# A two-layer attention encoder step on one core: full-width low weights for the sample, scans at another pace and place, and a scale chain in pieces

## The chip, the cores and the metric

The kernel runs on one core of a Trainium2 chip. The metric is device time in microseconds (us) of one execution. A core has five engines that run side by side, each in its own order: TensorE (PE, matmuls; its weight loads are listed as PEld), VectorE (DVE), ScalarE (ACT), GpSimd (POOL) and SyncE (SP), on whose queue this kernel starts all of its DMA transfers. SBUF is the on-chip memory of 128 partitions; PSUM takes what PE makes.

## The reference

Two layers, each `x + W_out(attention(RMSNorm(x)) * silu(gate))`, over a prompt of 2048 frames and a sample of 64 frames that comes with cached keys and values.

```python
def project(x, norm_g, w_in, q_g, k_g, n_heads, n_kv):
    h = rms_norm(x, norm_g)
    p = h @ w_in
    ...
    q, k, v, gate = jnp.split(p, [wq, wq + wkv, wq + 2 * wkv], axis=-1)
    ...
def gated_attention_layer(x_p, x_s, ck, cv, norm_g, w_in, q_g, k_g, w_out, ...):
    qp, kp, vp, gp = project(x_p, norm_g, w_in, q_g, k_g, n_heads, n_kv)
    op = prompt_band_attention(qp, kp, vp, past_chunks, bias_fn, sinks)
    y_p = x_p + (op * jax.nn.silu(gp)) @ w_out
    qs, ks, vs, gs = project(x_s, norm_g, w_in, q_g, k_g, n_heads, n_kv)
    os_, nk, nv = sample_band_attention(qs, ks, vs, ck, cv, bias_fn, sinks)
    y_s = x_s + (os_ * jax.nn.silu(gs)) @ w_out
```

D_MODEL is 1024; layer A has 16 heads over 2 key/value heads and a band of 2 past chunks of 64 frames, layer B 16 heads and 8 past chunks. The outputs must be near fp32 accuracy.

## The kernel before

**Precision by parts.** Each operand is split into a high and a low part, and a product is made of high x high, high x low and low x high. Layer A uses fp32r parts. Layer B and the second output projection use f16 parts, which need scales (powers of two) that keep weights, activations and outputs within f16. These scales are made from the largest absolute values of `w_in_b` (64 pieces), `w_o_b` (16) and `cv_b` (4).

**Scans.** The 84 pieces, 128 x 512 fp32 each (256 KB), are loaded one by one by `scan(n)` (line 155): a load on SP into one of two buffers `scan` (L162), and a DVE maximum into a column of `most` (L164). Calls stand in layer A's projections (35 scans) and, at 1 or 2 a call, five for every four calls, behind each residual add of layer A's output projection (the other 49). `behind(load, held["last"])` keeps a load behind the newest activation load on SP.

**Scale chain.** `scales()` (line 168) runs once, in the output projection's second half (`(half, j, m) == (1, 3, 0)`): it folds the norm gains into `most`, takes three maxima (`top`), transposes them by PE into one row of PSUM (L181), runs a dozen tiny DVE operations on that row (`scrow`, L188 to L207), spreads six results over the partitions with one PE matmul (L209), and copies them to `scl` (L210). `gsb` (L211) scales the weights of layer B (`wh` on ACT L396, `wl` on DVE L399). `C_B` and `G_B` are used from layer B's first projection on, `S_WO`, `S_OG` and `C_O` only in layer B's output projection.

**Projections.** A unit is 256 prompt frames (two tiles of 128) or the 64 sample frames. `project()` (line 576) runs eight chunks k of the contraction. A prompt tile takes three matmuls a chunk (L591, L592, L593). The sample's activations come as one stationary block of 128 columns, the 64 high parts beside the 64 low ones (`xl is None`): `xh x wh` with all 128 columns (L584, L587), and `xh[:, :64] x wl` with the 64 high columns alone (L585). The two halves of PSUM's partitions are added later. There are 13 sample projections: five in layer A (one of them 256 columns wide), eight in layer B.

**Output projection.** `output_jobs` (line 1508) walks two halves, eight jobs j of 264 frames, and four output groups m. A group is 24 matmuls (L1547, L1548, L1549) into one of two PSUM banks `pj`, then a DVE add of the residual (L1557; L1553 in layer B), for odd m a store (L1563, `x<-res`), and for layer A squares on ACT (L1493) summed by DVE (L1497, L1499). Each second group loads a residual (`res`, L1514); `xraw<-oga` (L458) brings the attention's output.

**Order.** PE's order is written out by hand: attention steps are followed by filler (projections and output jobs, as generators) up to hand-set marks. DVE, ACT, POOL and SP are ordered by the tile scheduler, which simulates the program and issues what its model holds ready first, so their order need not be that of the code.

Of the kernel before, what the change touches and what calls it, by code (L numbers as in the profile page):

```python
# [12 lines left out]
I32 = mybir.dt.int32  # L13
AF = mybir.ActivationFunctionType
ALU = mybir.AluOpType
AX = mybir.AxisListType

P = 128
D = 1024
KC = 8  # L20
# [33 lines left out]
def hybrid_encoder_kernel(  # L54
# [32 lines left out]
    nc = tc.nc  # L87
# [7 lines left out]
    def const(shape, name, dt=F32):  # L95
        return cp.tile(shape, dt, tag=name, name=name)
# [58 lines left out]
    def scan(n):  # L155
        for _ in range(n):
            i = len(scans)
            if i == NSCAN:
                return
            raw = t("scan", [P, 512], 2)  # L160
            dst = raw if i < 80 else raw.rearrange("p (e c) -> p e c", e=2)
            behind(load(dst, scan_source(i)).ins, held["last"])  # L162
            scans.append(raw)
            nc.vector.tensor_reduce(  # L164
                most[:, i : i + 1], raw, axis=AX.X, op=ALU.max, apply_absolute_value=True
            )

    def scales():
        assert len(scans) == NSCAN
# [4 lines left out]
        top = const([P, 4], "top")  # L174
        for j, (a, b) in enumerate(((0, 64), (64, 80), (80, 84))):
            nc.vector.tensor_reduce(
                top[:, j : j + 1], most[:, a:b], axis=AX.X, op=ALU.max, apply_absolute_value=True
            )
        ps = psum("tp", 512, 1)
        for j in range(3):  # L180
            nc.tensor.transpose(ps[0:1, j * P : (j + 1) * P], top[:, j : j + 1], ident)  # L181
        row = const([P, 16], "scrow")[0:1]
        m, e, r, o = row[:, 0:3], row[:, 3:6], row[:, 6:9], row[:, 10:16]

        def times(dst, a, c):
            nc.vector.tensor_scalar(dst, a, c, 1.0, op0=ALU.mult, op1=ALU.mult)

        nc.vector.tensor_reduce(  # L188
            m, ps[0:1, 0 : 3 * P].rearrange("p (j q) -> p j q", j=3), axis=AX.X, op=ALU.max
        )  # L190
        nc.vector.tensor_scalar(m, m, 1e-12, 1.0, op0=ALU.max, op1=ALU.mult)
# [3 lines left out]
        nc.vector.tensor_scalar(e.bitcast(I32), m.bitcast(I32), 0x7F800000, None, op0=ALU.bitwise_and)  # L195
        nc.vector.reciprocal(r, e)
        times(o[:, 0:1], r[:, 0:1], WB_)
        times(o[:, 1:2], e[:, 0:1], 1 / (HB * WB_))
        times(o[:, 2:3], e[:, 0:1], 0.5 / (VB * PB))
# [8 lines left out]
        ps = psum("tp", 512, 1)  # L208
        nc.tensor.matmul(ps[:, 0:6], ones[0:1, 0:1].to_broadcast([1, P]), o, start=True, stop=True)  # L209
        nc.vector.tensor_copy(scl[:, 0:6], ps[:, 0:6])  # L210
        nc.vector.tensor_scalar(gsb, gain[:, 1, :], S_W, 1.0, op0=ALU.mult, op1=ALU.mult)  # L211
# [364 lines left out]
    def project(tile_, xc, w, C, res, ps=None):  # L576
        tt, t0, n = tile_
        ps = ps or psum("pj", 512, 2)
        for k in range(KC):
            wh, wl = weights_of(w, k)  # L580
            xh, xl = xc.parts[k // 2]
            if xl is None:
                if k == 0:
                    nc.tensor.matmul(ps[:, :C], xh[:, k % 2, :], wh, start=True, stop=False)  # L584
                nc.tensor.matmul(ps[:n, :C], xh[:, k % 2, :n], wl, start=False, stop=False)  # L585
                if k > 0:
                    nc.tensor.matmul(ps[:, :C], xh[:, k % 2, :], wh, start=False, stop=k == KC - 1)  # L587
# [221 lines left out]
    def layer_a():  # L809
# [4 lines left out]
        def add_unit(qd, place, unit):  # L814
# [79 lines left out]
            def gen():  # L894
# [8 lines left out]
                for it in mine:  # L903
# [12 lines left out]
                    if qd:  # L916
                        scan(1 if it is mine[-1] or qd == 3 else 0)
# [230 lines left out]
    def layer_b():  # L1148
# [4 lines left out]
        def add_unit(hp, unit):  # L1153
# [21 lines left out]
            def gen():  # L1175
# [5 lines left out]
                for e, (tt, t0, n) in enumerate(tiles):  # L1181
# [24 lines left out]
                    it.ready = e == len(tiles) - 1  # L1206
                    yield c
# [300 lines left out]
    def output_jobs(layer, half, xin, xout):  # L1508
# [15 lines left out]
        def add_unit(j):  # L1524
# [11 lines left out]
            def gen():  # L1536
                oc = st.x.pop(j)
                w = st.w
                for m in range(4):
# [16 lines left out]
                    else:  # L1556
                        nc.vector.tensor_tensor(rv[:, m % 2], ps[:, :OT], rv[:, m % 2], op=ALU.add)  # L1557
                        if (half, j, m) == (1, 3, 0):
                            scales()
                        else:  # L1560
                            scan(1 + (m == 0))
# [140 lines left out]
```

## Time and profile before

| | us |
|---|---|
| median of 3 runs (lowest, highest) | 2261.91 (2259.24, 2263.51) |
| the profiled execution | 2259.01 |
| its span | 2257.2 |
| busy: PE / DVE / ACT / POOL | 2188.9 / 1692.5 / 1425.9 / 717.3 |
| DVE maxima `most<-scan` (84 of 684 ns) | 57.4 |
| DVE idle just before them | 52.1 |
| mean granted TensorE clock | 0.992 |

Layer A's projections and attention fill the span up to about 655 us, its output projection 655 to 890, layer B up to about 2040, and the second output projection the rest. Of the 84 scans, the first starts at 218.4 us and the last maximum ends at 808.8.

How to read it: a matmul's shown duration includes its way through the array, and the next one starts before it ends, so the distance from start to start tells the pace. "Idle before" is time in which an engine had nothing to run, with what ended it; only PE's own idle time lengthens a stage in which PE sets the pace. In rows of waits the columns are total, times and longest wait. In rows of stages they are the stretch, its length, busy time and count of each engine, the granted TensorE clock as a share, the share of the DMA engines and GB/s.

### The profile page before, as it was taken

The numbers are of one execution on the slowest core, as the hardware profiler recorded it, in microseconds if no ns is written. First come the engines' busy times: TensorE is split into PE (matmuls) and PEld (weight loads), VectorE is DVE, ScalarE is ACT, GpSimd is POOL, SyncE is SP. The second block draws the span as 40 slices with busy tenths as digits, with TensorE's granted clock in tenths as the row PEclk, the third lists the DMA queues.
The fourth block names the chain that finished last, engine by engine and source line by source line (L and its number), as shares of the span: only waits on it lengthen the run. The fifth ranks groups of instructions, "written<-read, shape, count | busy, mean of one in ns | idle before, by whom it ended". The sixth has DMA issues, their size and how long they took to land.

```text
span 2257.2 us, 42504 instructions
## 1 busy us (share of the span) xinstructions
PE 2188.9 (97%) x13908; PEld 1651.0 (73%) x13908; DVE 1692.5 (75%) x5505; ACT 1425.9 (63%) x3610; POOL 717.3 (32%) x1022
## 2 busy tenths in 40 slices
PE   8999999999999899999999999999999999999999
PEld 7887888878878898566666666666666666667888
DVE  7889988888886555888687777777767778777543
ACT  7888777776774333566676666766666666666321
POOL 5654533333344345652222222222222222221000
PEclk9999999999999999999999999999999999999999
DMA  8946546855457876433232232332423323233665
GB/s 280 290 147 217 179 149 210 241 181 175 168 166 234 260 230 188 135 121 122 72 119 81 80 103 86 94 96 64 121 79 93 97 70 118 81 87 119 185 191 157
DMA packets 244894, 332.19 MB, mean 147 GB/s; under 512 B 26096, under 2 KB 165760, under 8 KB 244640
## 3 DMA queue, kind: packets, MB, share of 16 engines
q1 hardware_dynamic: 244672, 329.47, 47.2%
q8 instruction: 109, 1.79, 0.3%
q14 instruction: 113, 0.93, 0.1%
HBM read 257.59 MB, written 73.43 MB: 147 GB/s over the span
## 4 chain that ended last, share of the span: by engine, by line
PE 68%; DVE 14%; DMA 7%; ACT 7%; issue 4%; POOL 1%; SPq 0%; ACTq 0%; POOLq 0%; DVEq 0%
PE pj L591 11%; PE pj L593 11%; PE pj L592 11%; PE sb L742 5%; PE o L1391 4%; PE pj L1547 4%; PE pj L1549 3%; PE pj L1548 3%; PE tp L742 3%; PE sb L1297 2%; PE sb L1296 2%; DMA scan<-in_w_in_b_dram 2%; PE sa L742 2%; DVE sq L669 1%; DVE p L1300 1%
## 5 line engine op out<-in xcount | busy, mean ns | idle before, releaser
L591 PE MATMUL pj<-wh,xx 128*128 128x512 f16 (+2 forms) x1648 | 639.4, 388 | 1.3 <-ACT wh L396 0.8
L592 PE MATMUL pj<-wl,xx 128*128 128x512 f16 (+2 forms) x1648 | 623.8, 379 | 4.7 <-DVE wl L399 4.7
L593 PE MATMUL pj<-wh,xx 128*128 128x512 f16 (+2 forms) x1648 | 624.4, 379 | 0.6 <-POOL xx L478 0.6
L673 POOL TENSOR_TENSOR f<-f,mhalf 128x4 f32<-128x4 f32 (+3 forms) x221 | 224.5, 1017 | 412.1 <-DVE f L669 405.4
L1304 ACT ACTIVATE p<-p,nm 128x640 f32<-128x640 f32 (+5 forms) x264 | 199.3, 755 | 228.5 <-DVE nm L1300 227.3
L1547 PE MATMUL pj<-xx,wh 128*128 128x264 f32 (+1 forms) x1024 | 293.1, 286 | 12.1 <-DVE res L1557 8.8
L1549 PE MATMUL pj<-xx,wl 128*128 128x264 f32 (+1 forms) x1024 | 289.2, 282 | 3.0 <-DVE wl L392 2.6
L1548 PE MATMUL pj<-xx,wh 128*128 128x264 f32 (+1 forms) x1024 | 289.4, 283 | 0.0
L718 DVE SCALAR_TENSOR_TENSOR pl<-sb,ph 128x640 f16<-128x640 f32 (+4 forms) x256 | 188.8, 738 | 130.7 <-ACT ph L717 130.1
L1144 POOL TENSOR_TENSOR o<-gt,o 128x256 f32<-128x256 f32 (+1 forms) x132 | 103.0, 780 | 382.7 <-ACT p L1052 78.8
L1300 DVE CUSTOM_DVE_ANT_0 p<-sb,BT 128x640 f32<-128x640 f32 (+5 forms) x272 | 196.5, 722 | 34.7 <-PE sb L1297 27.7
L742 PE MATMUL sb<-ident,p 128*128 128x128 f32 x1144 | 205.6, 276 | 10.8 <-DVE nm L1300 4.8
L478 POOL TENSOR_TENSOR xx<-xraw,xx 128x528 fp32r<-128x528 f32 (+4 forms) x144 | 179.5, 1266 | 103.0 <-ACT xx L477 63.2
L1052 ACT ACTIVATE p<-p,nm 128x257 f32<-128x257 f32 (+2 forms) x272 | 134.6, 498 | 106.0 <-DVE nm L1046 97.9
L742 PEld LDWEIGHTS sb<-ident,p 128*128 128x128 f32 x1144 | 149.0, 141 | 63.2 <-ACT sq L686 10.7
L593 PEld LDWEIGHTS <-xx 128*128 128x128 f16 x1024 | 100.5, 98 | 125.0 <-issue 4.2
L717 ACT ACTIVATE ph<-sb 128x640 f16<-128x640 f32 (+4 forms) x256 | 160.8, 628 | 46.2 <-PE sb L742 44.4
L669 DVE CUSTOM_DVE_ANT_0 sq<-pa 128x64 f32<-128x64 f32 (+1 forms) x834 | 169.8, 251 | 13.0 <-ACT pa L614 11.0
L591 PEld LDWEIGHTS <-xx 128*128 128x128 f16 x1024 | 100.1, 98 | 76.3 <-issue 1.4
L592 PEld LDWEIGHTS <-xx 128*128 128x128 f16 x1024 | 100.9, 99 | 68.0 <-issue 2.2
L1391 PE MATMUL o<-pl,values 128*128 128x256 f16 (+1 forms) x672 | 149.0, 255 | 0.0
L1391 PEld LDWEIGHTS <-values 128*128 128x128 f16 x1344 | 133.3, 100 | 16.2
(255 smaller groups left out, 5053.5 us busy)
## 6 DMA issues: line engine op xcount, KB each, us to landing
xx<-xsb SPq DMA_DIRECT2D x224, 256.0 KB, 2.7
xx<-xsa SPq DMA_DIRECT2D x88, 512.0 KB, 4.9
xraw<-oga SPq DMA_DIRECT2D x64, 264.0 KB, 4.0
xraw<-ogb SPq DMA_DIRECT2D x64, 264.0 KB, 3.5
xsa<-xx SPq DMA_DIRECT2D x32, 512.0 KB, 4.2
scan<-in_w_in_b_dram SPq DMA_DIRECT2D x64, 256.0 KB, 4.3
wraw<-in_w_in_b_dram SPq DMA_DIRECT2D x64, 256.0 KB, 3.0
xraw<-in_x_dram SPq DMA_DIRECT2D x40, 256.0 KB, 4.2
```

What stands on the lines that cost most here:

```text
L591: nc.tensor.matmul(ps[:n, :C], xh, wh, start=k == 0, stop=False)
L592: nc.tensor.matmul(ps[:n, :C], xh, wl, start=False, stop=False)
L593: nc.tensor.matmul(ps[:n, :C], xl, wh, start=False, stop=k == KC - 1)
L669: nc.vector.tensor_tensor_reduce(out=sq[:n, c], in0=src[:, c], in1=src[:, c], op0=ALU.mult, op1=ALU.add, scale=1.0, scalar=HD * EPS, accum ...
L673: nc.gpsimd.tensor_tensor(fv, fv, mhalf[:n, :H], op=ALU.pow)
L742: nc.tensor.transpose(out, in_, ident[:n, :n])
L1300: mi = nc.vector.tensor_tensor_reduce(out=p[r, :nk], in0=S[r, o : o + nk], in1=b, op0=ALU.add, op1=ALU.min, scale=1.0, scalar=3e38, accum_ ...
L1304: ex = nc.scalar.activation(p[:n, :nk], p[:n, :nk], AF.Exp, scale=-1.0, bias=it.nm[:n, c : c + 1], accum_out=it.sm[:n, c : c + 1],)
L1391: nc.tensor.matmul(it.O[:, h * T + q0 : h * T + q1_], vt, p[:, c, q0:q1_], start=start, stop=stop)
L1547: nc.tensor.matmul(ps[:, :OT], wh, oh, start=k == 0, stop=False)
L1548: nc.tensor.matmul(ps[:, :OT], wh, ol, start=False, stop=False)
L1549: nc.tensor.matmul(ps[:, :OT], wl, oh, start=False, stop=k == KC - 1)
```

## The change

1. In `project()`, the sample's `wl` matmuls take all 128 columns, as the `wh` ones do, and each chunk issues `wh` and then `wl`. The low x low product comes in as well.
2. `scan(n, end)` first takes the maximum of the load issued by the call before, then issues its own load, and stops at `end`. Up to scan 64 it runs in layer A and in the first half of the output projection, now one scan a call; the 20 scans of `w_o_b` and `cv_b` run in layer B, head pairs 1 and 2.
3. The scale chain is cut in six: `input_top`, `input_across` and `input_scales` in the output projection's second half, behind groups (j, m) = (0, 0), (0, 2) and (1, 0), which give `S_W`, `C_B`, `G_B` and `gsb`; `output_top`, `output_across` and `output_scales` in layer B, head pair 3, units 0, 1 and 2.

```diff
-    def scan(n):
+    def scan(n, end=NSCAN):
         for _ in range(n):
             i = len(scans)
-            if i == NSCAN:
+            if i and scans[i - 1] is not None and (i < end or i == end):
+                raw, scans[i - 1] = scans[i - 1], None
+                nc.vector.tensor_reduce(
+                    most[:, i - 1 : i], raw, axis=AX.X, op=ALU.max, apply_absolute_value=True
+                )
+            if i >= end:
                 return
             raw = t("scan", [P, 512], 2)
             dst = raw if i < 80 else raw.rearrange("p (e c) -> p e c", e=2)
             behind(load(dst, scan_source(i)).ins, held["last"])
             scans.append(raw)
-            nc.vector.tensor_reduce(
-                most[:, i : i + 1], raw, axis=AX.X, op=ALU.max, apply_absolute_value=True
-            )
...
+    def across(a, b):
+        ps = psum("tp", 512, 1)
+        for j in range(a, b):
+            nc.tensor.transpose(ps[0:1, j * P : (j + 1) * P], top[:, j : j + 1], ident)
+        nc.vector.tensor_reduce(
+            m[:, a:b], ps[0:1, a * P : b * P].rearrange("p (j q) -> p j q", j=b - a), axis=AX.X, op=ALU.max
+        )
+        nc.vector.tensor_scalar(m[:, a:b], m[:, a:b], 1e-12, 1.0, op0=ALU.max, op1=ALU.mult)
...
+    def everywhere(a, b):
+        ps = psum("tp", 512, 1)
+        nc.tensor.matmul(
+            ps[:, a:b], ones[0:1, 0:1].to_broadcast([1, P]), o[:, a:b], start=True, stop=True
+        )
+        nc.vector.tensor_copy(scl[:, a:b], ps[:, a:b])
...
+    def input_across():
+        across(0, 1)
+        powers(0, 1)
+        times(o[:, 0:1], r[:, 0:1], WB_)
+        times(o[:, 1:2], e[:, 0:1], 1 / (HB * WB_))
+        times(o[:, 2:3], e[:, 0:1], 0.5 / (VB * PB))
+
+    def input_scales():
+        everywhere(0, 3)
+        nc.vector.tensor_scalar(gsb, gain[:, 1, :], S_W, 1.0, op0=ALU.mult, op1=ALU.mult)
...
             xh, xl = xc.parts[k // 2]
             if xl is None:
-                if k == 0:
-                    nc.tensor.matmul(ps[:, :C], xh[:, k % 2, :], wh, start=True, stop=False)
-                nc.tensor.matmul(ps[:n, :C], xh[:, k % 2, :n], wl, start=False, stop=False)
-                if k > 0:
-                    nc.tensor.matmul(ps[:, :C], xh[:, k % 2, :], wh, start=False, stop=k == KC - 1)
+                nc.tensor.matmul(ps[:, :C], xh[:, k % 2, :], wh, start=k == 0, stop=False)
+                nc.tensor.matmul(ps[:, :C], xh[:, k % 2, :], wl, start=False, stop=k == KC - 1)
...
                     if qd:
-                        scan(1 if it is mine[-1] or qd == 3 else 0)
+                        scan(1 if it is mine[-1] or qd == 3 else 0, 64)
...
+                    if hp in (1, 2):
+                        scan(1)
+                    step = {(3, 0): output_top, (3, 1): output_across, (3, 2): output_scales}
+                    if e:
+                        step.get((hp, u), lambda: None)()
                     yield c
...
-                        if (half, j, m) == (1, 3, 0):
-                            scales()
-                        else:
-                            scan(1 + (m == 0))
+                        if half == 0:
+                            scan(1, 64)
+                        step = {(1, 0, 0): input_top, (1, 0, 2): input_across, (1, 1, 0): input_scales}
+                        step.get((half, j, m), lambda: None)()
```

`powers` masks the exponent and takes the reciprocal; `largest` takes the maxima of `most`; the three `output_` pieces do with columns 1 and 2 of the row what the old function did. The new functions shift the lines below them: L584 to L587 become L616 and L617, the maximum L164 becomes L160, the scan's load L162 becomes L167, the residual add L1557 becomes L1592, the scores' minimum L1300 becomes L1335.

**PE, the second sample projection of layer B.** Before (`wh` rows are L584 and L587, `wl` rows L585; the size is that of the result):

```order
L584 LDWEIGHTS xx_14988
L584 MATMUL pj_15253<-wh_13164,xx_14988 128x512
L585 LDWEIGHTS xx_14988
L585 MATMUL pj_15253<-wl_13165,xx_14988 64x512
L585 LDWEIGHTS xx_14988
L585 MATMUL pj_15253<-wl_13192,xx_14988 64x512
L587 LDWEIGHTS xx_14988
L587 MATMUL pj_15253<-wh_13191,xx_14988 128x512
```

With the change:

```order
L616 LDWEIGHTS xx_14954
L616 MATMUL pj_15225<-wh_13095,xx_14954 128x512
L617 LDWEIGHTS xx_14954
L617 MATMUL pj_15225<-wl_13096,xx_14954 128x512
L616 LDWEIGHTS xx_14954
L616 MATMUL pj_15225<-wh_13122,xx_14954 128x512
L617 LDWEIGHTS xx_14954
L617 MATMUL pj_15225<-wl_13123,xx_14954 128x512
```

The number of matmuls and of weight loads is the same; only the width and the order within a chunk changed.

**DVE, the first half of layer A's output projection.** Scans are numbered in the order of their loads; each `res<-pj` row is the residual add of one group, and `BT` rows are the sums of squares. Before, one job:

```order
L164 TENSOR_REDUCE most<-scan_9888 128x1
L1557 TENSOR_TENSOR res_9848<-pj_9850,res_9848 128x264
L164 TENSOR_REDUCE most<-scan_9891 128x1
L1557 TENSOR_TENSOR res_9848<-pj_9894,res_9848 128x264
L1497 TENSOR_TENSOR BT<-p_9924 128x264
L164 TENSOR_REDUCE most<-scan_9920 128x1
L1557 TENSOR_TENSOR res_9927<-pj_9929,res_9927 128x264
L164 TENSOR_REDUCE most<-scan_9955 128x1
L164 TENSOR_REDUCE most<-scan_9984 128x1
L1557 TENSOR_TENSOR res_9927<-pj_9958,res_9927 128x264
```

With the change:

```order
L160 TENSOR_REDUCE most<-scan_10059 128x1
L1592 TENSOR_TENSOR res_9989<-pj_10032,res_9989 128x264
L1532 TENSOR_TENSOR BT<-p_10062 128x264
L160 TENSOR_REDUCE most<-scan_10094 128x1
L1592 TENSOR_TENSOR res_10065<-pj_10067,res_10065 128x264
L160 TENSOR_REDUCE most<-scan_10123 128x1
L1592 TENSOR_TENSOR res_10065<-pj_10096,res_10065 128x264
L1532 TENSOR_TENSOR BT<-BT,p_10126 128x264
L1534 TENSOR_TENSOR BT<-BT,p_10126 128x264
L160 TENSOR_REDUCE most<-scan_10203 128x1
```

Five maxima for four adds became four for four. In the code `scan_10094` is loaded behind the add of `pj_10067` and its maximum now follows one call later; the scheduler set that maximum ahead of the same add, where it stood before.

**DVE, layer B, head pair 1, about 1066 us into the profile of before.** With the change, where before `o` (the sample's output) was followed straight by L1300, the scores' minimum:

```order
L1402 TENSOR_TENSOR o_2859_14000<-o_13993,o_2859_14000 64x64 x2
L160 TENSOR_REDUCE most<-scan_13955 128x1
L160 TENSOR_REDUCE most<-scan_14068 128x1
L1335 ISA p_14023,nm_13885<-sb_14022,BT 128x640
L1335 ISA nm_13885 128x1
L1293 CAST q_2861_14017<-q_2861_14017 64x256 x2
```

Two maxima stand ahead of the minimum. The 20 maxima of layer B stand in ten such pairs, one a unit.

49 lines of the change are left out of this document (24 added, 25 removed).

## The prediction

> **What bounds the kernel now.** I read the page first, then busy time by stage, then what TensorE itself waited for, then the timeline where the edit lies. The profiled execution took 2259.0 us, its span 2257.2; that lies 2.9 under the 2261.9 median of the runs shown, and all sums below are made against 2259.0.
>
> ```profile
> span 2257.2 us, 42504 instructions
> PE 2188.9 (97%) x13908; PEld 1651.0 (73%) x13908; DVE 1692.5 (75%) x5505; ACT 1425.9 (63%) x3610; POOL 717.3 (32%) x1022
> ```
>
> PE sets the pace, so a change is worth what it takes out of PE's sequence or PE's waits. The stages (columns: stretch, length, busy time and count of each engine, granted clock, DMA share, GB/s):
>
> ```profile
> 655.00:700.00 45.00, 42.19 (x315) 39.67 (x316) 37.23 (x98) 31.29 (x86) 21.19 (x29) 0.96 0.57 175
> 700.00:840.00 140.00, 127.36 (x984) 123.33 (x983) 77.35 (x156) 46.27 (x77) 57.02 (x48) 0.98 0.80 250
> 840.00:880.00 40.00, 40.00 (x333) 40.00 (x332) 20.07 (x37) 11.24 (x18) 19.95 (x20) 1.00 0.59 174
> 1215.00:2030.00 815.00, 807.80 (x5002) 528.99 (x5000) 610.28 (x2136) 533.86 (x1356) 192.47 (x290) 1.00 0.30 90
> ```
>
> From 700 to 880 PE does layer A's output projection, one kind of matmul. At 840 to 880 nothing disturbs it: 333 in 40 us, 0.120 us each. The 984 of 700 to 840 should have taken 118 us and took 140, so 22 us were lost there, more than the busy column shows, since a matmul's shown duration covers a lost start; the granted clock of 0.98 accounts for at most 2.8 of them. Layer B (1215 to 2030) is 99% busy. PE's own waits, first 700 to 840, then two of the three of 1040 to 2037 (total, times, longest):
>
> ```profile
> PE pj L1547 <- DVE res L1557: 6.8, 9, 1.4
> PE tp L209 <- DVE scrow L207: 3.2, 1, 3.2
> PE pj L1549 <- DVE wl L392: 2.6, 4, 1.1
> ```
>
> ```profile
> PE sb L742 <- ACT sq L686: 3.3, 5, 0.7
> PE sb L742 <- DVE nm L1300: 2.3, 6, 0.4
> ```
>
> **Part 1: 128 columns for the sample's low weights.** It touches 13 projections: five in layer A (fp32r) and eight in layer B (f16). First a prompt projection of layer B, then a sample projection in layer B, then one in layer A (start, duration, instruction):
>
> ```profile
> 1006.07 0.38 PE L591 MATMUL pj<-wh,xx 128*128 128x512 f16 x1
> 1006.29 0.38 PE L592 MATMUL pj<-wl,xx 128*128 128x512 f16 x1
> 1006.50 0.38 PE L593 MATMUL pj<-wh,xx 128*128 128x512 f16 x1
> ...
> 1008.40 0.38 PE L584 MATMUL pj<-wh,xx 128*128 128x512 f16 x1
> 1008.71 0.62 PE L585 MATMUL pj<-wl,xx 128*64 128x512 f16 x2
> 1009.26 0.39 PE L587 MATMUL pj<-wh,xx 128*128 128x512 f16 x1
> 1009.58 0.40 PE L585 MATMUL pj<-wl,xx 128*64 128x512 f16 x1
> 1009.91 0.39 PE L587 MATMUL pj<-wh,xx 128*128 128x512 f16 x1
> ```
>
> ```profile
> 628.99 0.39 PE L585 MATMUL pj<-wl,xx 128*64 128x512 f32 x1
> 629.21 0.39 PE L587 MATMUL pj<-wh,xx 128*128 128x512 f32 x1
> 629.44 0.39 PE L585 MATMUL pj<-wl,xx 128*64 128x512 f32 x1
> ```
>
> The number to read is start to start. Full-width f16 matmuls follow each other by 0.215 us; where 128 columns turn to 64 or back it is 0.32 to 0.33, so 0.11 us a change of width. In one projection the order is wh, wl, wl, wh, wl, wh ...: 14 changes, 14 x 0.11 = 1.54 us. Where another instruction stands between, the change was paid as well. Eight projections of layer B: 12.3 us. In layer A the same alternation runs at 0.22 to 0.23 and costs nothing, so nothing is gained there. The new matmuls have the same moving 512 columns, so they cost 0.215 each. Lower end: what is saved may come back as a wait elsewhere, but the PE waits above show 5.6 us over all of layer B's 1000 us; I keep 9 as the low end, 12.3 as the high one, and take 12.
>
> The weight loads go the same way as the pace in f16: the narrow one is not cheaper.
>
> ```profile
> L585 PEld LDWEIGHTS <-xx 128*64 128x64 f16 x64 | 6.2, 106 | 11.9 <-issue 10.0
> L587 PEld LDWEIGHTS <-xx 128*128 128x128 f16 x56 | 5.4, 96 | 14.2 <-issue 14.2
> ```
>
> [...]
>
> **Part 2: scans in the output projection.** A scan is a 256 KB load and one DVE maximum. The load's two buffers form a ring. The rows of 700 to 800 (duration min/median/max in ns; microseconds to landing), the waits of 700 to 840, and one stall:
>
> ```profile
> L164 DVE TENSOR_REDUCE most<-scan x35: 674/686/689, 702.0 to 798.2; 128x1 f32<-128x512 f32 x35
> ...
> DMA to landing us min/median/max: 2.4/4.3/5.9
> ```
>
> ```profile
> DVE most L164 <- DMA scan<-in_w_in_b_dram: 19.1, 17, 2.7
> DVE most L164 <- DMA scan<-in_w_o_b_dram: 15.8, 15, 3.1
> ```
>
> ```profile
> 718.20 0.69 DVE L164 TENSOR_REDUCE most<-scan 128x1 f32<-128x512 f32 x1 [2.58 <-DMA scan<-in_w_in_b_dram]
> 718.80 0.42 DVE L1557 TENSOR_TENSOR res<-pj,res 128x264 f32<-128x264 f32 x1
> ```
>
> ```profile
> 719.28 0.39 PE L1547 MATMUL pj<-xx,wh 128*128 128x264 f32 x1 [1.42 <-DVE res L1557]
> ```
>
> DVE sits at the maximum until the load lands, the residual add behind it is late, and PE, with two pj banks, waits for the add. A group m is 24 matmuls, 2.88 us. Before, five scans fall on four groups: a buffer's turn (two scans) has 2 x 0.8 x 2.88 = 4.6 us, but landing and maximum need 4.3 + 0.69 = 5.0. The ring is overbooked and sets PE's pace. Now one scan falls on a group: a turn has 5.8 us. That rate, not the lag, is what I count on. The order of the change shows that the lag is taken back: the scheduler still sets each maximum just ahead of an add, as before. With slow landings (5.9 + 0.69 = 6.6) a turn is still too short, and the second pj bank covers up to a group. The SP queue loses one load in five there, and all of them in the second half; x stores, res and xraw loads behind them on SP go out sooner.
>
> The price: of the 22 us, 2.6 are the wl waits and 3.2 the scale chain; about 15 hang on the scans, with the slow restarts behind each wait. I take 12 of them (low 5, high 16). Counted from 640 on, two more such waits come in:
>
> ```profile
> PE pj L1547 <- DVE res L1557: 8.8, 11, 1.4
> ```
>
> For these I take 1.5. The wl waits at the start of the second half come from four weight chunks split just in time, which stays; only the DVE maxima ahead of them go: 1 (0 to 2.6).
>
> **Part 3: the scale chain.** Before, PE's order has the three transposes and the broadcast matmul back to back, and PE stands idle until DVE has gone from the first to the last of these:
>
> ```profile
> 824.58 0.54 DVE L188 TENSOR_REDUCE scrow<-tp 1x3 f32<-1x384 f32 x1
> ...
> 826.16 0.14 DVE L207 TENSOR_TENSOR scrow<-scrow 1x1 f32<-1x1 f32 x1
> ```
>
> Now whole groups lie between transposes and matmul; seven small operations of some 0.15 us hide under a group's 2.88. I take 3.3 us (3.2 of wait, and the restart; low 2). If gsb came late, ACT's wh would wait, and behind them its squares and xx casts:
>
> ```profile
> ACT wh L396 <- DVE gsb L211: 6.1, 1, 6.1
> ```
>
> ACT had that wait before, at the same kind of place, without a PE wait on xx, so it costs nothing here either. What is late next is PE's own pace.
>
> **Part 4: what moves into layer B.** 20 loads, 20 maxima, two transposes, one matmul and a dozen tiny DVE operations. On SP the loads stand among xx loads, at a DMA share of 0.30. On DVE the maxima come in ten pairs, some straight ahead of the scores' minimum L1300, behind which stand the exponential and PE's transposes. The reserve there (end of the exponential to the transposes' start):
>
> ```profile
> 1057.70 0.83 ACT L1304 ACTIVATE p<-p,nm 128x640 f32<-128x640 f32 x1 [2.08 <-DVE nm L1300]
> ...
> 1192.02 0.83 ACT L1304 ACTIVATE p<-p,nm 128x640 f32<-128x640 f32 x1 [1.81 <-DVE nm L1300]
> ```
>
> ```profile
> 1062.73 0.71 PE L742 MATMUL sb<-ident,p 128*128 128x128 f32 x5
> ...
> 1195.06 0.71 PE L742 MATMUL sb<-ident,p 128*128 128x128 f32 x5
> ```
>
> 4.2 us in the one, 2.2 in the other. A pair delays DVE by 2 x 0.69 = 1.4 us if the loads have landed, and by 4.5 if the first waits the longest time seen (3.1). So a pair costs PE 0 to 2.3 us, ten pairs 0 to 23. The DMA is far idler here than in the stage whose 3.1 that is, so I take 0.2 a pair, 2 us. PE's three extra instructions are 0.5, in it.
>
> Sum: -12 - (12 + 1.5 + 1) - 3.3 + 2 = -28.8; 2259.0 - 28.8 = 2230. Against the median the same saving gives 2233; I say 2232.
>
> **The rivals.**
> - *The stall stays*: since the maxima stay ahead of the adds, each slow landing still holds the add, PE at full pace loads the DMA more, and only 4 of the 14.5 come back: 2241 to 2244. For it: the unchanged order, 0.80 DMA share. Against: 4.6 against 5.8 us a turn. 17%.
> - *The PE saving is given back*: layer B is held by ACT and DVE next, and the faster sample projection only lengthens waits: 2259 - 18 + 2 = 2243. Against: 5.6 us of waits in 1000. 5%.
> - *Layer B's pairs become the new wait*, the case on the other side: if both maxima of a pair wait for their landing, DVE is held 1.4 + 2 x 3.1 = 7.6 us, 5.4 beyond the smaller reserve; it decides from 2.9 us of PE loss a pair (29 in all), a hold of some 5 us. At 3.5 a pair: 2259 - 31 + 35 = 2263. For it: two loads issued together behind xx loads, DVE strictly in order. Against: both buffers are free by then and landings are short at a DMA share of 0.30. Past 2.9: 5%; between 1 and 2.9 (2240 to 2258): 8%.
> - *A change of width costs in layer A too*: 5 x 1.54 = 7.7 more, 2224. The fp32r rows speak against it: 4%. [...]
>
> **How the numbers follow.** My forecast (2223 to 2240) has 61%. No change I call within 0.2% (4.5 us), about what a measurement of this kernel can tell. Faster by more: the forecast, the first two rivals, layer A's, and most of the middle pair case, 92%; same 4%; slower 4%. The range for 8 in 10: the low end is all terms at their best, 2259 - 12.3 - 22 - 2 = 2223; the high end holds the first two rivals and a loss of 1.5 us a pair: 2248.
>
> **What would show it.** Part 1: sample matmuls in layer B at 0.215 start to start, every weight load near 96 ns. Part 2: 700 to 840 loses its waits of L1547 for the residual add, and the stage runs near 0.120 us a matmul; DVE may still wait at maxima without PE waiting. Part 3: no PE wait at the broadcast matmuls. Part 4: waits of PE on nm or pl in layer B rise by no more than 2 to 3 us. I would be wrong if the 64-column price were not the width's but the place's, or if PE's waits in 1040 to 1215 grew by tens of us.

## The result: no change, and the profile after

The changed kernel took 2260.49 us (median of 12 runs, 2256.5 to 2264.73) beside 2259.87 us of the kernel before (12 runs, 2255.67 to 2264.72): a ratio of 1.0002 with a 95% interval of 0.9993 to 1.0012. The prediction was 2232 us with a range of 2223 to 2248. Nearly everything forecast to be gained is missing.

The profiled execution took 2260.59 us. First its span and busy time, from the page, then the stages (columns as before):

```profile
span 2258.8 us, 42506 instructions
...
PE 2173.3 (96%) x13910; PEld 1646.8 (73%) x13910; DVE 1700.0 (75%) x5510; ACT 1422.8 (63%) x3610; POOL 717.5 (32%) x1022
```

```profile
700.00:840.00 140.00, 129.19 (x1013) 126.64 (x1013) 75.81 (x136) 44.79 (x75) 59.75 (x50) 0.98 0.74 226
840.00:880.00 40.00, 40.00 (x333) 40.00 (x332) 20.89 (x40) 12.75 (x21) 21.89 (x22) 1.00 0.57 169
1040.00:1215.00 175.00, 166.73 (x1028) 107.84 (x1027) 135.53 (x462) 107.65 (x274) 37.81 (x59) 1.00 0.38 117
```

PE was busy 15.6 us less than before (2188.9) in a longer span: its work became shorter, and waits took the place. The output projection still starts only 1013 matmuls between 700 and 840, where the dense rate of 333 in 40 us would make 1166. And 1040 to 1215, where layer B's scans now stand, has 8.3 us without PE work.

PE does the same work in the same order in both kernels, so the start of each matmul can be set beside the start of the same matmul in the other trace. How the distance grows from stage to stage is the cleanest account of where time went; negative is gained (us, my own subtraction of start times; the stages are those of the kernel before):

| stage | forecast | measured |
|---|---|---|
| start to 655, layer A | 0 | +0.4 |
| 655 to 800, output projection, scans | -14.5 | -0.4 |
| 800 to 890, scale chain | -3.3 | -5.5 |
| 890 to 1040, first f16 sample projection | -1.5 | +0.5 |
| 1040 to 1215, scans of layer B, second sample projection | +0.5 | +9.4 |
| 1215 to 2037, six sample projections, second chain | -9.0 | -2.8 |
| 2037 to the end | 0 | 0.0 |

(The forecast's 12 us for the eight projections are spread over the last three stages of layer B, 1.5 each; the 2 us for its pairs are in the fifth row.)

What PE waited for, first at 700 to 840, then at 1040 to 2037 (total, times, longest):

```profile
PE pj L1582 <- DVE res L1592: 8.5, 8, 1.8
```

```profile
PE sb L772 <- DVE pl L748: 11.5, 16, 1.4
...
PE tp L772 <- DVE scrow L187: 0.7, 1, 0.7
PE tp L772 <- DVE scl L203: 0.4, 1, 0.4
```

The wait for the residual adds, 6.8 us before, is still there. The wait of the score transposes (L772) for `pl` (L748, the low part that DVE makes of transposed scores) was 0.4 us before; it is the new one. The two `tp` rows are the second scale chain.

**The output projection.** SP's own waits at 700 to 770, the kernel before and then the changed one:

```profile
SPq L1514 <- DMA x<-res: 15.1, 10, 2.6
SPq L162 <- DMA scan<-in_w_in_b_dram: 7.5, 6, 3.1
SPq L162 <- DVE res L1557: 7.5, 9, 1.0
...
SPq L162 <- DMA scan<-in_w_o_b_dram: 1.3, 1, 1.3
```

```profile
SPq L1549 <- DMA x<-res: 29.1, 8, 5.0
...
SPq L167 <- DVE res L1592: 1.7, 4, 0.7
```

Before, SP waited 16.3 us ahead of scan loads (L162), read here as the wait for a buffer of the scans to come free, and 15.1 us ahead of residual loads (L1514), for the store of `x` from the same buffer to land. With one scan a group the first wait is nearly gone, as forecast, and the second has taken over its time. One round of it, from SP's timeline, then DVE's and PE's:

```profile
720.50 0.42 SPq L1598 DMA_DIRECT2D x<-res  x1
725.77 0.37 SPq L1549 DMA_DIRECT2D res<-in_x_dram  x1
...
726.75 0.41 SPq L167 DMA_DIRECT2D scan<-in_w_in_b_dram  x1
```

```profile
731.09 0.69 DVE L160 TENSOR_REDUCE most<-scan 128x1 f32<-128x512 f32 x1 [1.95 <-DMA scan<-in_w_in_b_dram]
731.70 0.42 DVE L1592 TENSOR_TENSOR res<-pj,res 128x264 f32<-128x264 f32 x1
```

```profile
732.18 0.39 PE L1582 MATMUL pj<-xx,wh 128*128 128x264 f32 x1 [1.31 <-DVE res L1592]
```

The store is issued at 720.5, and the residual load behind it holds SP's queue until it has landed; only then does the scan's load start; its maximum starts 4.3 us later, the add follows, and PE has waited 1.31 us. Not all of these 5 us on the queue count: the scan's buffer came free only at 724.3, when the maximum of the load before the last one ended, so the load started 2.5 us late. From 700 to 770 the 19 scan loads started 1.9 us on average after their buffer came free, and their maxima 4.6 us after the load (my own subtraction); with 0.69 for the maximum a turn of a buffer took 7.1 us. The forecast counted landing and maximum, 5.0 us, and left out the queue.

**Layer B.** The same place before (DVE, then PE) and with the change (DVE, then PE):

```profile
1066.58 0.82 DVE L1300 CUSTOM_DVE_ANT_0 p<-sb,BT 128x640 f32<-128x640 f32 x1
...
1070.06 0.82 DVE L718 SCALAR_TENSOR_TENSOR pl<-sb,ph 128x640 f16<-128x640 f32 x1
```

```profile
1071.47 0.27 PE L742 MATMUL sb<-ident,p 128*128 128x128 f32 x1
```

```profile
1061.90 0.69 DVE L160 TENSOR_REDUCE most<-scan 128x1 f32<-128x512 f32 x1 [0.35 <-DMA scan<-in_w_o_b_dram]
1062.76 0.69 DVE L160 TENSOR_REDUCE most<-scan 128x1 f32<-128x512 f32 x1 [0.17 <-DMA scan<-in_w_o_b_dram]
1063.48 0.82 DVE L1335 CUSTOM_DVE_ANT_0 p<-sb,BT 128x640 f32<-128x640 f32 x1
...
1066.95 0.82 DVE L748 SCALAR_TENSOR_TENSOR pl<-sb,ph 128x640 f16<-128x640 f32 x1
```

```profile
1067.92 0.30 PE L772 MATMUL sb<-ident,p 128*128 128x128 f32 x1 [1.28 <-DVE pl L748]
```

From the minimum to `pl` both take 3.5 us. The pair (0.35 + 0.69 + 0.17 + 0.69 = 1.9 us) moves both back. Before, `pl` ended at 1070.88 and the transposes started at 1071.47, a reserve of 0.6 us; 1.9 less 0.6 is 1.3, and PE waits 1.28 us. The transposes write PSUM space that `pl` has to read first: in the code scores and transposes take turns in the two `sb` buffers.

**The sample projections.** PE in layer B, half of the fourth f16 one:

```profile
1302.14 0.39 PE L616 MATMUL pj<-wh,xx 128*128 128x512 f16 x1
1302.37 0.38 PE L617 MATMUL pj<-wl,xx 128*128 128x512 f16 x1
1302.58 0.38 PE L616 MATMUL pj<-wh,xx 128*128 128x512 f16 x1
1302.80 0.38 PE L617 MATMUL pj<-wl,xx 128*128 128x512 f16 x1
1303.69 0.33 PE L772 MATMUL sb<-ident,p 128*128 128x128 f32 x1 [0.51 <-DVE pl L748]
```

Start to start is 0.215 us, the price forecast; and then, in the middle of the projection, PE comes to the transposes too early for `pl` and waits 0.51 us. They start 0.67 us later than the pace would have them (1303.69 against 1302.80 + 0.215). The same place before, DVE and PE:

```profile
1298.31 0.81 DVE L718 SCALAR_TENSOR_TENSOR pl<-sb,ph 128x640 f16<-128x640 f32 x1
```

```profile
1299.18 0.33 PE L742 MATMUL sb<-ident,p 128*128 128x128 f32 x1
```

`pl` ended at 1299.12, so the reserve was 0.06 us, and no wait was shown. A saving that comes back as such a wait is called the give-back below.

### The profile page after: what moved, and what is told of

Read it like the earlier page. It is cut to its first block, busy times and chain, and to the rows that moved or that the text cites. A ratio compares the mean times of both kernels' runs of the same rounds, so it can differ in the third digit from the quotient of the medians.

```text
span 2258.8 us, 42506 instructions
## 1 busy us (share of the span) xinstructions
PE 2173.3 (96%) x13910; PEld 1646.8 (73%) x13910; DVE 1700.0 (75%) x5510; ACT 1422.8 (63%) x3610; POOL 717.5 (32%) x1022
## 4 chain that ended last, share of the span: by engine, by line
PE 52%; DVE 14%; DMA 5%; ACT 5%; issue 4%; SPq 1%; POOL 1%; POOLq 0%; ACTq 0%; DVEq 0%
PE pj L621 8%; PE pj L623 8%; PE pj L622 8%; PE sb L772 4%; PE pj L1582 4%; PE o L1426 4%; PE pj L1584 4%; PE pj L1583 4%; PE sb L1332 2%; PE sb L1331 2%; DVE p L1335 2%; PE tp L772 2%; DVE pl L748 2%; DMA scan<-in_w_in_b_dram 2%; DMA x<-res 1%
## 5 line engine op out<-in xcount | busy, mean ns | idle before, releaser
L703 POOL TENSOR_TENSOR f<-f,mhalf 128x4 f32<-128x4 f32 (+3 forms) x221 | 223.8, 1014 | 418.6 <-DVE f L699 411.6
L748 DVE SCALAR_TENSOR_TENSOR pl<-sb,ph 128x640 f16<-128x640 f32 (+4 forms) x256 | 188.9, 738 | 125.9 <-ACT ph L747 125.3
L772 PE MATMUL sb<-ident,p 128*128 128x128 f32 x1144 | 206.0, 276 | 22.5 <-DVE pl L748 13.3
L1335 DVE CUSTOM_DVE_ANT_0 p<-sb,BT 128x640 f32<-128x640 f32 (+5 forms) x272 | 196.5, 723 | 27.7 <-PE sb L1332 20.6
L772 PEld LDWEIGHTS sb<-ident,p 128*128 128x128 f32 x1144 | 148.5, 141 | 80.6 <-DVE pl L748 23.0
```

The costliest lines, as they stand in the source:

```text
L703: nc.gpsimd.tensor_tensor(fv, fv, mhalf[:n, :H], op=ALU.pow)
L748: b = nc.vector.scalar_tensor_tensor(dst_lo, src, scale, wide(dst_hi), op0=ALU.mult, op1=ALU.subtract)
L772: nc.tensor.transpose(out, in_, ident[:n, :n])
L1335: mi = nc.vector.tensor_tensor_reduce(out=p[r, :nk], in0=S[r, o : o + nk], in1=b, op0=ALU.add, op1=ALU.min, scale=1.0, scalar=3e38, accum_ ...
```

## The experiments

Each kernel ran beside the kernel before. The table gives the ratio to that kernel with its 95% interval, and the matmul-by-matmul stages as above (us against the profiled execution of the kernel before).

| run | median us | ratio (95%) | to 655 | 655-800 | 800-890 | 890-1040 | 1040-1215 | 1215-2037 |
|---|---|---|---|---|---|---|---|---|
| the change | 2260.49 | 1.0002 (0.9993-1.0012) | +0.4 | -0.4 | -5.5 | +0.5 | +9.4 | -2.8 |
| wide_only | 2252.43 | 0.9961 (0.9947-0.9974) | +1.0 | +0.7 | -0.9 | -0.4 | -0.5 | -5.2 |
| narrow_rest | 2269.72 | 1.0026 (1.0013-1.0038) | +6.5 | -3.7 | -5.5 | -1.1 | +10.5 | +2.3 |
| noscan | 2245.44 | 0.9921 (0.9896-0.9945) | +0.3 | -16.4 | -5.5 | -1.9 | +9.6 | -2.9 |
| lag | 2253.48 | 0.9964 (0.9950-0.9978) | +1.5 | -13.7 | -5.5 | +0.8 | +9.8 | -2.9 |
| before_lag | 2261.15 | 1.0002 (0.9992-1.0013) | +1.6 | +0.5 | +1.9 | -0.6 | 0.0 | 0.0 |
| scanq_scalar | 2254.45 | 0.9973 (0.9962-0.9985) | +23.3 | -17.0 | -4.3 | +1.1 | -0.5 | -2.1 |
| scanq_out | 2256.59 | 0.9980 (0.9966-0.9993) | +1.0 | -4.5 | -5.5 | +1.3 | +10.1 | -2.6 |
| bnm | 2255.55 | 0.9974 (0.9963-0.9986) | +3.9 | -2.0 | -5.5 | +0.3 | +4.6 | -2.8 |
| both_places | 2243.82 | 0.9924 (0.9909-0.9938) | -1.8 | -10.5 | -5.5 | +1.5 | +4.2 | -3.0 |
| half1 | 2239.79 | 0.9917 (0.9895-0.9939) | start to 890: -13.3 | | | +0.5 | -0.5 | -4.1 |
| copy_pool | 2250.53 | 0.9944 (0.9926-0.9962) | +5.5 | -2.3 | -5.5 | +0.2 | +4.7 | -6.7 |
| half1_copy | 2230.68 | 0.9868 (0.9852-0.9884) | start to 890: -11.9 | | | 0.0 | -1.1 | -8.4 |

Layer A moves by up to 6 us from one profiled execution to another (narrow_rest, copy_pool) with nothing changed there that would explain it. 655 to 800 moves by about 3: the change, narrow_rest, bnm and copy_pool have the same scans there and show -0.4, -3.7, -2.0 and -2.3. 890 to 1040 moves by about 3 as well (-1.9 to +1.5), and so does what comes after 2037 (-3.4 to +3.4, not listed); 1040 to 1215 and 1215 to 2037 repeat within 0.7 us. The medians carry all of this as noise, so the verdicts go by stages, and in the first output projection by the ratios as well.

**wide_only: the sample's columns alone.**

An edit of the kernel before.

```diff
-                if k == 0:
-                    nc.tensor.matmul(ps[:, :C], xh[:, k % 2, :], wh, start=True, stop=False)
-                nc.tensor.matmul(ps[:n, :C], xh[:, k % 2, :n], wl, start=False, stop=False)
-                if k > 0:
-                    nc.tensor.matmul(ps[:, :C], xh[:, k % 2, :], wh, start=False, stop=k == KC - 1)
+                nc.tensor.matmul(ps[:, :C], xh[:, k % 2, :], wh, start=k == 0, stop=False)
+                nc.tensor.matmul(ps[:, :C], xh[:, k % 2, :], wl, start=False, stop=k == KC - 1)
```

> Only the 128-column sample matmuls are put into the kernel before. Theory: each of the eight f16 sample projections becomes about 1.6 us shorter on PE, but six or more of them give some 0.6 us back at once, because the score transposes in the middle of the projection then come before DVE has read the bank they write to; net 0.9 to 1.0 us each, 7 to 8 us in all: 2252 to 2253, ratio about 0.9967. Rival, the prediction's term: nothing is given back, 12.3 us, 2247.5, ratio 0.9946. [...]

Measured: 2252.43 us, as expected. Each projection from the third on gains 0.87 us and the first nothing: it gains 1.55 us until 1014 and loses 1.56 until 1040, as PE comes to the next unit's `xx` too early (it waits 2.0 us for it there, 0.5 before). In all of layer B 6.1 us, half of the forecast's 12. PE's waits from 1035 to 2035:

```profile
PE sb L739 <- DVE pl L715: 3.7, 9, 0.5
```

So the give-back is there without any scan in layer B. Layer A: no gain (+1.0 us to 655, where the fourth rival's price, 5 x 1.54, would have given -7.7).

**narrow_rest: all of the change but the sample's columns.**

The changed kernel with `project()` of the kernel before.

```diff
-                nc.tensor.matmul(ps[:, :C], xh[:, k % 2, :], wl, start=False, stop=k == KC - 1)
+                nc.tensor.matmul(ps[:n, :C], xh[:, k % 2, :n], wl, start=False, stop=False)
...
```

> The changed kernel with the 64-column sample matmuls put back, so only the scans and the scale chain are changed. Theory: the chain gives 5.5 us, the output projection's scans nothing, ten pairs of maxima in layer B cost 8 to 10 us and the scale steps there 1 to 2: 5 to 7 us slower than the kernel before, 2265 to 2267, ratio 1.0025. Rival: the pairs' price in the changed kernel belongs to the faster sample projections (PE arriving too early), and without them the pairs cost under 3 us: 2257 or less.

Measured: 2269.72 us, above the 2265 to 2267 expected; in the profiled execution 6.5 us of the time are layer A's drift. 1040 to 1215 costs 10.5 us with the slow sample matmuls too, and PE's wait for `pl` there is 7.4 us (8.0 in the changed kernel). The pairs' price is their own. The second scale chain costs 2.3.

**noscan: no scans in the output projection.** 29 loads and maxima of `w_in_b` are left out (the trace has 35 of the 64 loads; the expectation says 28).

```diff
+    def skip():
+        n = len(scans)
+        if n < 64:
+            scan(1, n)
+            nc.vector.memset(most[:, n:64], 0.0)
+            scans.extend([None] * (64 - n))
...
                         if half == 0:
-                            scan(1, 64)
+                            skip()
```

> The changed kernel without any scan in layer A's output projection: 28 loads and maxima of w_in_b are left out (their columns of most are set to zero), the rest stays. Theory (the maxima ahead of the residual adds are what holds the adds): PE's waits for the residual adds between 655 and 800 us fall from 10 us to under 2, and the time by 8 to 11 us against the changed kernel: 2250 to 2252. Rival (the loop on SP of x store landing, residual load and next store sets the pace by itself): at least 5 us of these waits stay, and the gain is under 5 us.

Measured: 2245.44 us, 16.0 us less in 655 to 800 than the changed kernel, and 14.3 less than the mean of the four executions named above; more than the 8 to 11 expected. PE no longer waits for residual adds, and the stage has 1136 matmuls:

```profile
700.00:840.00 140.00, 138.78 (x1136) 138.17 (x1135) 69.54 (x121) 49.49 (x82) 66.43 (x56) 1.00 0.67 204
```

So the forecast's sum (about 15 us hang on the scans) was right about what is there to gain. The store and the residual load alone do not hold PE, though SP still waits 24.9 us for the landing of `x` stores at 700 to 770.

**lag: maxima behind the adds.**

```diff
-                nc.vector.tensor_reduce(
+                r = nc.vector.tensor_reduce(
...
+                if "add" in held and i < 64:
+                    behind(r.ins, held["add"])
...
-                        nc.vector.tensor_tensor(rv[:, m % 2], ps[:, :OT], rv[:, m % 2], op=ALU.add)
+                        held["add"] = nc.vector.tensor_tensor(rv[:, m % 2], ps[:, :OT], rv[:, m % 2], op=ALU.add).ins
```

> The changed kernel with the lag enforced in the output projection: each maximum is ordered behind the residual add after which the code takes it, so that it no longer stands ahead of that add. Theory (place of the maximum ahead of the add): PE's waits for residual adds at 655 to 800 us fall from 10 us to under 4, time 6 to 10 us less than the changed kernel: 2250 to 2255. Rival (the loads come too late for any place): the next add is held in place of this one, waits stay over 7 us and the time within 3 us of the changed kernel.

Measured: 2253.48 us; 13.3 us less in the stage than the changed kernel. That is the most it can be: the profiled execution was the fastest of its nine, the ratios differ by 0.38%, 8.6 us, and both_places below has -10.5 in the stage, 8.4 less than the mean of the four. I count 8 to 13 us. PE's and DVE's waits, 655 to 800:

```profile
PE pj L1584 <- DVE res L1594: 2.0, 3, 1.6
```

```profile
DVE most L160 <- DMA scan<-in_w_in_b_dram: 20.7, 16, 2.4
```

DVE still waits 20.7 us for the scans (26.0 in the changed kernel), and PE waits 2.0 us for the adds in place of 10.0. SP still waits 32.1 us for the landing of `x` stores at 700 to 770. Only the place of the maximum differs.

**before_lag: the same place at the old rate.** The kernel before, five scans for four groups, each maximum taken one call later by `take(i)`, which orders it behind the add.

```diff
     def scan(n):
+        if "add" in held:
+            for i in range(len(scans)):
+                if scans[i] is not None:
+                    take(i)
...
-            nc.vector.tensor_reduce(
-                most[:, i : i + 1], raw, axis=AX.X, op=ALU.max, apply_absolute_value=True
-            )
+            if "add" not in held:
+                take(i)
```

> The kernel before with its rate of five scans for four groups kept, but each maximum taken one call later and ordered behind the residual add there. Theory (the place ahead of the add costs the time, not the rate): PE's waits for residual adds at 655 to 800 us fall from 8.8 us to under 3 and the time by 9 to 13 us: 2247 to 2251, ratio 0.995. Rival (the prediction's: at five scans for four groups two buffers are overbooked, so any place is late): waits stay over 6 us, gain under 4 us.

Measured: 2261.15 us, no gain; PE waits for the adds at 655 to 822:

```profile
PE pj L1559 <- DVE res L1569: 10.0, 7, 3.9
```

My theory fell here, and the forecast was half right about the rate: 23 of the 47 scan loads from 655 on start within 0.1 us of their buffer coming free in this trace (19 in the kernel before), and at 700 to 770 load to maximum and the maximum take 5.2 us, more than the 4.6 of a turn. I read this as two buffers overbooked, so that a place one group later is late again; the longest wait grew from 1.4 us to 3.9. What the runs show is that the rate had to fall and the maximum had to move: the rate alone gives 0.4 to 3.7 us, the place alone nothing.

**scanq_scalar: the scans' loads on another queue.**

```diff
-            behind(load(dst, scan_source(i)).ins, held["last"])
+            nc.scalar.dma_start(dst, scan_source(i))
```

> The changed kernel with the scans' loads started on ScalarE's queue instead of SyncE's; maxima stay ahead of the adds. Theory (loads are late because they stand on SP behind a residual load that waits for an x store to land): DVE's waits for the scans at 655 to 800 us fall from 26 us to under 12 and PE's waits for the adds from 10 us to under 4; 5 to 10 us less than the changed kernel: 2251 to 2256. Rival (the landing itself, 4 to 5 us at this DMA load, and the two buffers make them late): waits of DVE over 20 us, time within 3 us of the changed kernel.

Measured: 2254.45 us, and not the question asked. With the order behind the activation loads gone, the scheduler put all 84 scans into layer A's first 300 us:

```profile
L160 DVE TENSOR_REDUCE most<-scan x84: 646/680/689, 4.0 to 296.0; 128x1 f32<-128x512 f32 x84
```

It prices the stages that lose them: 655 to 800 gains 16.6 us against the changed kernel, 1040 to 1215 gains 9.9, and layer A pays 22.9.

**scanq_out: another queue in the output projection alone.**

```diff
-            behind(load(dst, scan_source(i)).ins, held["last"])
+            if "sq" in held and i < 64:
+                behind(nc.scalar.dma_start(dst, scan_source(i)).ins, held["sq"])
+            else:
+                behind(load(dst, scan_source(i)).ins, held["last"])
```

> The changed kernel with the loads of the scans in the output projection alone started on ScalarE's queue, two at a time right behind the square of each pair of groups (a pair of maxima then stands ahead of every second residual add); all other scans as in the changed kernel. Theory (the loads are late because they stand on SP behind a residual load that waits for an x store to land): with the loads issued early, DVE's waits for them at 655 to 800 us fall from 26 us to under 8 and PE's waits for the adds from 10 us to under 4, though every maximum still stands ahead of an add: 7 to 12 us less than the changed kernel, 2248 to 2253. Rival (the landing under this DMA load is too long for two buffers): DVE's waits over 15 us, gain under 4 us.

Measured: 2256.59 us. In the stage it is 4.1 us less than the changed kernel, but only 0.8 less than narrow_rest, so the stage says little; PE's waits for the adds fall from 10.0 us to 4.8, between the two theories, and DVE's for the scans stay, as the rival has it. 655 to 800:

```profile
PE pj L1585 <- DVE res L1595: 4.8, 7, 1.0
```

```profile
DVE most L160 <- DMA scan<-in_w_in_b_dram: 22.8, 16, 2.4
```

Past SP's queue the loads still come late, because here each pair starts only behind the square of the adds before it, and lands 4 to 5 us later. No run starts the loads early past SP's queue, so how much of the lateness the queue makes is read from the trace and not shown by a run. At one scan a group, lag shows what makes lateness cost PE: the maximum ahead of the add.

**bnm: layer B's maxima singly, behind the minima.** `take` is the maximum of one scan, `scan_load` its load alone.

```diff
             bg.anchor(mi, ex)
+            for q in pending()[:1]:
+                take(q, mi.ins)
...
                     if hp in (1, 2):
-                        scan(1)
+                        scan_load()
```

> The changed kernel with layer B's maxima taken singly, each ordered behind a scores' minimum, where the code of the attention comes by, instead of in pairs. Theory (a pair delays DVE's pl, which frees the bank for the next transposes, by more than its small reserve): PE's waits for pl at 1035 to 1215 us fall from some 9 us to under 3, time 6 to 10 us less than the changed kernel: 2251 to 2255. Rival (the loads and other work of these units cost it, wherever the maxima stand): within 3 us of the changed kernel.

Measured: 2255.55 us; 1040 to 1215 costs 4.6 us in place of 9.4, a gain of 4.8 where 6 to 10 were expected. PE at 1035 to 1215:

```profile
PE sb L795 <- DVE pl L771: 3.0, 6, 0.8
```

The scheduler set some of the maxima ahead of a minimum again (of the first seven, three, and one ahead of `pl`), so the rest of the price may well be the same price; PE's wait for `pl` there is 3.0 us, after 8.0.

**both_places: lag and bnm together.** No edit of its own.

> The changed kernel with both repairs: maxima behind the adds in the output projection and singly behind the minima in layer B. If the two are independent, their gains add: 12 us and 6 to 9 us, 2240 to 2243, ratio to the kernel before 0.991 to 0.992. If one only uncovers the other's wait, no more than 14 us together: 2246 or more.

Measured: 2243.82 us, just past the 2240 to 2243 expected: the stages give 10.1 and 5.2 us against the changed kernel, so the two add within the noise.

**half1: no scans in layer B at all.** With the lag; the 20 last scans and the second chain in the output projection's second half.

```diff
-                        if half == 0:
-                            scan(1, 64)
+                        scan(1, NSCAN if half else 64)
-                        step = {(1, 0, 0): input_top, (1, 0, 2): input_across, (1, 1, 0): input_scales}
+                        step = {
+                            (1, 0, 0): input_top, (1, 0, 2): input_across, (1, 1, 0): input_scales,
+                            (1, 5, 2): output_top, (1, 6, 0): output_across, (1, 6, 2): output_scales,
+                        }
...
-                    if hp in (1, 2):
-                        scan(1)
-                    step = {(3, 0): output_top, (3, 1): output_across, (3, 2): output_scales}
...
```

> The changed kernel with the maxima behind the adds, and with the 20 scans of w_o_b and cv_b and the second scale chain moved from layer B into the output projection's second half, one scan a group. Theory: layer B's pairs and its scale steps are gone (9.4 and 2.1 us), and in the second half nothing new is waited for: 22 to 24 us less than the changed kernel, 2236 to 2239, ratio to the kernel before 0.990. Rival: the second half takes over what layer B gives back, as PE's waits for the adds there rise by 5 us or more: 2243 or more.

Measured: 2239.79 us, just past the 2236 to 2239 expected. Layer B's 1040 to 1215 is back to -0.5, and the second half of the output projection takes the scans almost unseen: PE waits for adds 2.7 us in all of 655 to 870, none of it after 800.

```profile
PE pj L1579 <- DVE res L1589: 2.7, 5, 0.9
```

**copy_pool: 0.59 us less on DVE ahead of `pl`.**

```diff
-                        nc.vector.tensor_copy(q1[hh][halves[1 - hh]], q1[hh][rows].bitcast(F32))
+                        nc.gpsimd.tensor_copy(q1[hh][halves[1 - hh]], q1[hh][rows].bitcast(F32))
```

> The changed kernel with one of DVE's operations between a scores' minimum and pl, the copy of q into the other 64 partitions (0.59 us for two in layer B), moved to GpSimd. Theory (the wait at each sample projection, 0.5 us, and part of each pair's price are DVE's lateness with pl, which frees the bank): PE's waits for pl at 1035 to 2035 us fall from 11.5 us to 3 to 6, time 5 to 9 us less than the changed kernel. Rival (GpSimd's copy is slower and delays the next scores, or the wait has another cause): within 3 us of the changed kernel, or slower.

Measured: 2250.53 us; layer B from 1040 on is 8.6 us shorter than in the changed kernel. PE's waits at 1020 to 2035 fall from 13.2 us to

```profile
PE sb L772 <- DVE pl L748: 4.4, 15, 0.7
```

8.8 us less, so the give-back of the sample projections and the price of the pairs are one thing: when DVE comes to `pl`.

**half1_copy: the last two together.** It beats both kernels.

> The last two together: maxima behind the adds, no scans in layer B, copy of q on GpSimd. Theory: what is left of the sample projections' give-back (some 4 us) goes as well, 3 to 5 us less than the kernel of the second run of these: 2232 to 2235, ratio to the kernel before 0.988. Rival: no better than that run.

Measured: 2230.68 us, a ratio of 0.9868 (0.9852 to 0.9884) to the kernel before.

## Why the prediction was wrong, point by point

- *What bounds the kernel.* Right as far as the runs go: the stages that lost time are those in which PE's waits grew.
- *Part 1, 12 us.* The price of a change of width was right (0.215 us start to start now, 1.55 to 1.6 us a projection), in f16 alone: in layer A it is 0.23 still, and the rival with a price there too fell.

```profile
628.32 0.39 PE L617 MATMUL pj<-wl,xx 128*128 128x512 f32 x1
628.55 0.40 PE L616 MATMUL pj<-wh,xx 128*128 128x512 f32 x1
```

  The lower end of 9 was wrong: half is given back (6.1 us in wide_only). The step that failed took the 5.6 us of PE waits in layer B for the size of the danger. A wait of zero says only that PE is not early; the reserve behind `pl` was 0.06 us at the place shown, and a saving of 0.8 us in front of the transposes met it at once (0.67 us lost). The rival had this at 5% as all or nothing.
- *Part 2, 13.5 us.* The step "That rate, not the lag, is what I count on" failed. The rate did what was said of it (SP's waits for a scan buffer fell from 16.3 to 1.7 us), but the turn of 5.8 against 5.0 us had no room for the load's time on SP's queue behind a residual load that waits for a store: a turn took 7.1 us. I had seen in the order that the maxima stay ahead of the adds, and that was the point: lag gives 8 to 13 us with DVE still waiting 20.7 us for the scans, before_lag gives nothing at the old rate. The rival "the stall stays", at 17%, is what happened; its sum kept 4 of 14.5 us (the wl waits among them), and the run kept 0.4 (2.1 on average over the four executions with these scans). The size of the prize was right (14 to 16 us in noscan).
- *The wl waits, 1 us.* Of 2.6 us 2.3 stay, now put down to `wh` and `wl`.
- *Part 3, 3.3 us.* Right in kind, 5.5 us in size: the wait is gone, and with it 3.6 us at a granted clock of 0.53 behind it (below). Against wide_only, whose execution had the wait without that stretch, it is 4.6.
- *Part 4, 2 us.* Mis-sized: 9.4 to 10.5 us for ten pairs, and 2.1 to 2.3 for the second chain, which I had at 0.5. The reserve was measured at the wrong place, from the exponential's end to the transposes' start. The transposes do not wait for `p` alone, but for their bank, which `pl` frees, and `pl` stands 3.5 us behind the minimum in DVE's order. The sign named for it, PE's waits on nm or pl rising by 2 to 3 us at most, was missed by far (11.5 us for `pl`, after 0.4). The pair case past 2.9 us did not come: the loads had nearly landed (0.35 and 0.17 us in the pair shown, 6.7 us for all twenty scans, the longest 1.3), as argued.

- *The sum.* Its terms, -12 - 14.5 - 3.3 + 2, make -27.8; -28.8 was written, a slip of 1 us that decides nothing; the pairs' rival has it too (31 for 29.8).

What came out, -0.4 and -5.5 in the output projection, +0.5, +9.4 and -2.8 in layer B, adds up to 1.2 us: the result.

## What to carry to other kernels

A reserve is read from the last of everything that the waiting instruction needs, the bank it writes among it, not from its data alone (here 4.2 and 2.2 us by the data, 0.6 and 0.06 by the bank, at four places); and where no wait is shown, the reserve may be nothing, as at the last of these. When a queue is freed of one wait, the next one in it may take the time, as on SP here (the wait for a scan buffer fell from 16.3 to 1.7 us, the one for the store of `x` rose from 15.1 to 29.1): add up the whole loop (store, landing, load, landing, use) before a rate is called low enough. And an order that the code asks for must be looked up in what the scheduler made of it: here the side work belonged behind the operation that PE waits for, and had to be tied there (8 to 13 us in lag).

## What the runs showed of the hardware that was not expected

The first chain's wait cost more than its length. In the profiled execution of the kernel before PE idled 3.19 us at it, and the next 3.6 us ran at a granted clock of 0.53 (18 matmuls in 3.6 us):

```profile
826.60:830.20 3.60, 3.60 (x18) 3.58 (x19) 2.47 (x5) 1.95 (x3) 0.00 (x0) 0.53 0.37 113
```

In wide_only PE idled 3.19 us at the same place (up to 828.7), and the clock behind it was full:

```profile
829.00:833.00 4.00, 4.00 (x34) 4.00 (x34) 2.88 (x7) 2.12 (x4) 0.10 (x1) 1.00 0.46 151
```

At a clock of 0.53, 3.6 us hold 1.7 us less work; wide_only gains 1.5 us on the kernel before from 822 to 832, with the same wait. So a wait of 3.19 us was followed by a clock of 0.53 in the one execution and by a full one in the other; the traces show that it happens, and not why.
